# A seven-product form for 3 of 8 pairs of k-tiles in the FFN input products of an encoder block

## The chip, the cores and the metric

The kernel runs on one core of one Trainium2 chip. The metric is the device time of one execution in microseconds, as the median of several runs. A profile of one further execution comes with it; it names the engines PE (TensorE, matmul), PEld (its weight loads), DVE (VectorE), ACT (ScalarE), POOL (GpSimd) and SP (SyncE, here the queue of most transfers).

## The reference

One layer of an encoder block on 256 tokens of width 2048, all float32. Three token mixers run on the normalized input: a dilated window attention, a grouped-query attention with rotary positions, and a cross attention into 256 memory tokens. Each branch is projected to the model width, weighted by a sigmoid gate, summed, projected by `w_o` and added to the input. Behind it stands the part that the change touches, the SwiGLU FFN with an inner width of 5632:

```python
hf = rms_norm(x, g_ffn[layer]) @ w_ffn_in[layer]
x = x + (jax.nn.silu(hf[..., :D_FF]) * hf[..., D_FF:]) @ w_ffn_out[layer]
```

`w_ffn_in` is 2048 x 11264; its left half (a) gives the gate, its right half (b) the value.

## The kernel before

**Number format.** TensorE multiplies in a reduced float32 form. To keep float32 accuracy every operand is split into a high part, rounded to that form, and a low part, the rest. `split` (L72) makes both: ACT copies to the high tile (L75), then DVE subtracts it from the source (L76). A product of two tiles is then three matmuls (L172 to L174): high by high, high by low, low by high.

**Tiling.** The 256 tokens are two row tiles (`T`, `t`) of 128. The model width is 16 k-tiles (`KT`) of 128. Weight columns come in tiles of 512 (`NC`), one PSUM bank wide. `product` (L150) multiplies all tokens by one column tile: it takes one bank per row tile, loads 4 k-tiles (1 MB, `raw`, 3 buffers) at a time on the SP queue (L146), splits them two k-tiles at a time into `whi` and `wlo` (4 buffers each), and issues for each k-tile and row tile the three matmuls, with the activations as the stationary operand and the weights streaming.

**Order.** The kernel is written as one program; a planner orders each engine's instructions at build time by priority (program order) and by its own estimate of when operands and buffers are ready. Each engine then runs its list strictly in order, waiting on semaphores. A buffer of a pool is taken when an earlier tile with the same tag is released.

**The stages.** Memory keys and values, the combined projections with the three attentions beside them, gates and branch projections, the `w_o` products, the FFN. In the `w_o` stage (L476) each of four column tiles is added to the residual `x` (L481), squared for the norm (L482), transposed by TensorE (`transposed`, L212, matmuls at L218), scaled by the gain and split into a quarter of `x1T`, the stationary operand of the FFN.

**The FFN.** Two blocks of column tiles, 6 and 5. For each of the 11 column tiles the kernel computes the product with a (L495), applies silu with the row scale of the norm on ACT (L498), computes the product with b (L499), multiplies on DVE (L501), transposes the result and splits it into `hT` (L505). After a block, four output products with `w_ffn_out` run over the block's `hT`, and DVE adds them to `x` (L513); behind the last block the rows go out.

**Memory.** The eight PSUM banks are two pools of 4: `pmm` for products and `pat` for transposes and attention. SBUF tiles of 8 KB per partition come from the pool `big` (11 buffers) and, from the last gate stage on, `tail` (4); those of 4 KB from `mid` (5).

Of the kernel before, what the change touches and what calls it, by code (L numbers as in the profile page):

```python
# [23 lines left out]
HD = 128  # L24
DFF = 5632
NC = 512
KF = DFF // P
PK, LOAD = 2, 4
# [18 lines left out]
MEM_SLOTS = [("kc", _i) for _i in range(4)] + [("vc", _i) for _i in range(4)]  # L47


@with_exitstack  # L50
def encoder_block(ctx: ExitStack, tc: tile.TileContext, a: dict, out: bass.AP):
    nc = tc.nc
    const = ctx.enter_context(tc.tile_pool(name="const", bufs=1))
    wp = ctx.enter_context(tc.tile_pool(name="wp", bufs=3))
# [4 lines left out]
    pmm = ctx.enter_context(tc.tile_pool(name="pmm", bufs=4, space=bass.MemoryType.PSUM))  # L59
    pat = ctx.enter_context(tc.tile_pool(name="pat", bufs=4, space=bass.MemoryType.PSUM))  # L60

    def s8(shape, name, dt=F32R, pool=None):
        return (pool or big).tile(shape, dt, name=name, tag="s8")

    def s4(shape, name, dt=F32):
        return mid.tile(shape, dt, name=name, tag="s4")

    def at_bank(name):
        return pat.tile([P, NC], F32, name=name, tag="at")


    def split(hi, lo, src, scale=None):  # L72
# [77 lines left out]
    def product(src, lhs, nk, head=(), beside={}):  # L150


        ps = [pmm.tile([P, NC], F32, name="mm") for _ in range(T)]
        k0 = 0
        while k0 < nk:
            n = head[0] if head else min(LOAD, nk - k0)
            head = head[1:]
            if k0 in beside:
                start(beside[k0])
            lhs(k0)  # L160
            raw = load(src, k0, n)
            for b in range(0, n, PK):
                m = min(PK, n - b)
                hi = wp.tile([P, PK, NC], F32R, name="whi", bufs=4)
                lo = wp.tile([P, PK, NC], F32R, name="wlo", bufs=4)
                split(hi[:, :m], lo[:, :m], raw[:, b:b + m])
                for i in range(m):
                    k = k0 + b + i
                    xh, xl = lhs(k)
                    for t in range(T):  # L170
                        c = slice(t * P, (t + 1) * P)
                        nc.tensor.matmul(ps[t], lhsT=xh[:, c], rhs=hi[:, i], start=(k == 0), stop=False)  # L172
                        nc.tensor.matmul(ps[t], lhsT=xh[:, c], rhs=lo[:, i], start=False, stop=False)  # L173
                        nc.tensor.matmul(ps[t], lhsT=xl[:, c], rhs=hi[:, i], start=False, stop=(k == nk - 1))  # L174
                    tick()
            k0 += n
        return ps
# [107 lines left out]
    headT, V = {}, {}  # L285
# [141 lines left out]
    r_m, r_x, r_f = (scales[:, i] for i in range(3))  # L427
# [61 lines left out]


    x1l = lambda k: (x1T[k // 4][:, 0, k % 4], x1T[k // 4][:, 1, k % 4])
    for c0, c1 in ((0, 6), (6, KF // 4)):
        hT = []
        for n in range(c0, c1):
            ap = product(a["w_ffn_a"][n], x1l, KT)  # L495
            sa = s4([P, T, NC], "sa")
            for t in range(T):
                nc.scalar.activation(sa[:, t], ap[t], AF.Silu, scale=r_f[:, 0, t:t + 1])  # L498
            bp = product(a["w_ffn_b"][n], x1l, KT)  # L499
            for t in range(T):  # L500
                nc.vector.scalar_tensor_tensor(sa[:, t], bp[t], r_f[:, 0, t:t + 1], sa[:, t],  # L501
                                               op0=ALU.mult, op1=ALU.mult)
            tl = s8([P, 2, 4, S], "hT", pool=tail if n % 6 < 4 and n < 6 or n > 8 else None)
            hT.append(tl)
            transposed([sa[:, t] for t in range(T)], lambda k, m: (tl[:, 0, k:k + m], tl[:, 1, k:k + m]))  # L505
        for n in range(4):
            op = product(a["w_ffn_out"][n][4 * c0 // PK:4 * c1 // PK],
                         lambda k: (hT[k // 4][:, 0, k % 4], hT[k // 4][:, 1, k % 4]), 4 * (c1 - c0))
            for t in range(T):
                for h in range(2 if c0 and n == 3 else 1):  # L510
                    w = NC if not (c0 and n == 3) else NC // 2
                    o = slice(n * NC + h * w, n * NC + (h + 1) * w)
                    nc.vector.tensor_add(x[t][:, o], op[t][:, h * w:(h + 1) * w], x[t][:, o])  # L513
                    if c0:
                        nc.sync.dma_start(out=out[t * P:(t + 1) * P, o], in_=x[t][:, o])


# [33 lines left out]
def _blocks(w):  # L551

    k, n = w.shape
    return w.reshape(k // P // PK, PK, P, n // NC, NC).transpose(3, 0, 2, 1, 4).reshape(n // NC, -1, P, PK * NC)


def _layout(i):
# [37 lines left out]
```

## Time and profile before

| | |
|---|---|
| median of 3 runs | 1437.51 us (1437.31 to 1438.21) |
| the profiled execution | 1438.22 us, of which the span is 1436.4 us |
| granted TensorE clock, mean | 0.998 |
| TensorE busy | 1416.7 us (99%), 6422 matmuls and transposes |
| VectorE busy | 781.2 us (54%) |
| ScalarE busy | 667.2 us (46%) |
| GpSimd busy | 78.8 us (5%) |
| moved by DMA | 276.98 MB, 193 GB/s over the span |
| FFN input products | 3 x 704 matmuls, 88 loads of 1 MB |

The span goes from the first to the last instruction of the profiled execution; the time of that execution is 1.8 us more. "Busy" adds up the durations of an engine's instructions. Matmuls overlap in the array, so that the duration of one is longer than the step from one to the next, and a TensorE that is shown as busy may still be slowed.

### The profile page before, as it was taken

The numbers are of one execution on the slowest core, as the hardware profiler recorded it, in microseconds if no ns is written. First come the engines' busy times: TensorE is split into PE (matmuls) and PEld (weight loads), VectorE is DVE, ScalarE is ACT, GpSimd is POOL, SyncE is SP. The second block draws the span as 40 slices with busy tenths as digits, with TensorE's granted clock in tenths as the row PEclk, the third lists the DMA queues.
The fourth block names the chain that finished last, engine by engine and source line by source line (L and its number), as shares of the span: only waits on it lengthen the run. The fifth ranks groups of instructions, "written<-read, shape, count | busy, mean of one in ns | idle before, by whom it ended". The sixth has DMA issues, their size and how long they took to land.

```text
span 1436.4 us, 16231 instructions
## 1 busy us (share of the span) xinstructions
PE 1416.7 (99%) x6422; PEld 1170.0 (81%) x6422; DVE 781.2 (54%) x912; ACT 667.2 (46%) x860; POOL 78.8 (5%) x146
## 2 busy tenths in 40 slices
PE   6999999999999999999999999999999999999998
PEld 4778788888888888888888888888888888888887
DVE  5677766744555555555644555545444445554543
ACT  6676555644444444444444444444333444444432
POOL 0013642200000000000000000000000000000000
PEclk9999999999999999999999999999999999999999
DMA  8876445465555556555555555565555555556562
GB/s 294 282 248 204 147 153 173 160 222 197 196 192 194 176 189 213 184 187 177 183 197 186 194 177 204 176 205 177 203 179 203 187 194 179 202 177 204 192 218 88
DMA packets 75772, 276.98 MB, mean 193 GB/s; under 512 B 5232, under 2 KB 7792, under 8 KB 75440
## 3 DMA queue, kind: packets, MB, share of 16 engines
q1 hardware_dynamic: 73248, 271.73, 56.0%
q10 hardware_dynamic: 2448, 4.22, 0.8%
q8 instruction: 50, 0.82, 0.2%
q14 instruction: 26, 0.21, 0.0%
HBM read 273.05 MB, written 2.88 MB: 192 GB/s over the span
## 4 chain that ended last, share of the span: by engine, by line
PE 92%; DMA 3%; POOL 2%; ACT 1%; issue 1%; DVE 1%; SPq 0%; ACTq 0%; DVEq 0%; POOLq 0%
PE mm L173 29%; PE mm L172 29%; PE mm L174 29%; PE tp L218 1%; DMA rawT<-in_xT 1%; DMA rows<-in_x 1%; DMA rows<-in_mem 1%; POOL rot L337 1%; POOL rot L340 1%; POOL rtmp L338 1%; ACT whi L75 0%; PE pT L396 0%; ACT rows L206 0%; PE hT L346 0%; POOL y L320 0%
## 5 line engine op out<-in xcount | busy, mean ns | idle before, releaser
L76 DVE TENSOR_TENSOR wlo<-raw,whi 128x1024 fp32r<-128x1024 f32 (+1 forms) x497 | 614.7, 1239 | 584.9 <-ACT whi L75 582.6
L75 ACT ACTIVATE whi<-raw 128x1024 fp32r<-128x1024 f32 (+1 forms) x497 | 525.5, 1061 | 642.6 <-PE mm L174 616.6
L174 PE MATMUL mm<-whi,x1T 128*128 128x512 f32 x704 | 274.8, 390 | 0.0
L172 PE MATMUL mm<-whi,x1T 128*128 128x512 f32 x704 | 274.8, 390 | 0.0
L173 PE MATMUL mm<-wlo,x1T 128*128 128x512 f32 x704 | 274.1, 389 | 0.0
L173 PE MATMUL mm<-wlo,xT 128*128 128x512 f32 x640 | 250.2, 391 | 1.0 <-DVE wlo L76 1.0
L172 PE MATMUL mm<-whi,xT 128*128 128x512 f32 x640 | 250.5, 392 | 0.1
L174 PE MATMUL mm<-whi,xT 128*128 128x512 f32 x640 | 249.5, 391 | 0.0
L173 PEld LDWEIGHTS mm<-wlo,x1T 128*128 128x128 f32 x704 | 132.2, 188 | 27.2
L174 PEld LDWEIGHTS mm<-whi,x1T 128*128 128x128 f32 x704 | 132.2, 188 | 27.1
L172 PEld LDWEIGHTS mm<-whi,x1T 128*128 128x128 f32 x704 | 132.2, 188 | 26.9
L173 PEld LDWEIGHTS mm<-wlo,xT 128*128 128x128 f32 x640 | 120.2, 188 | 26.1 <-DVE wlo L76 1.4
L172 PEld LDWEIGHTS mm<-whi,xT 128*128 128x128 f32 x640 | 120.1, 188 | 25.3 <-issue 0.8
L174 PEld LDWEIGHTS mm<-whi,xT 128*128 128x128 f32 x640 | 120.2, 188 | 24.4
L173 PE MATMUL mm<-wlo,hT 128*128 128x512 f32 x352 | 137.8, 391 | 0.0
L172 PE MATMUL mm<-whi,hT 128*128 128x512 f32 x352 | 137.7, 391 | 0.0
L174 PE MATMUL mm<-whi,hT 128*128 128x512 f32 x352 | 137.0, 389 | 0.0
L172 PEld LDWEIGHTS mm<-whi,hT 128*128 128x128 f32 x352 | 66.1, 188 | 14.4
L174 PEld LDWEIGHTS mm<-whi,hT 128*128 128x128 f32 x352 | 66.1, 188 | 14.3
L173 PEld LDWEIGHTS mm<-wlo,hT 128*128 128x128 f32 x352 | 66.1, 188 | 13.5
L173 PE MATMUL mm<-wlo,mT 128*128 128x512 f32 x128 | 50.8, 397 | 0.0
L172 PE MATMUL mm<-whi,mT 128*128 128x512 f32 x128 | 50.5, 395 | 0.0
(123 smaller groups left out, 997.5 us busy)
## 6 DMA issues: line engine op xcount, KB each, us to landing
raw<-in_w_gate SPq DMA_DIRECT2D x48, 1024.0 KB, 5.0
raw<-in_w_ffn_a SPq DMA_DIRECT2D x44, 1024.0 KB, 5.0
raw<-in_w_ffn_b SPq DMA_DIRECT2D x44, 1024.0 KB, 5.0
raw<-in_w_ffn_out SPq DMA_DIRECT2D x44, 1024.0 KB, 5.0
raw<-in_w_qkv SPq DMA_DIRECT2D x32, 1024.0 KB, 5.1
raw<-in_w_o SPq DMA_DIRECT2D x16, 1024.0 KB, 5.0
raw<-in_w_br SPq DMA_DIRECT2D x8, 1024.0 KB, 4.9
raw<-in_w_mem SPq DMA_DIRECT2D x15, 512.0 KB, 4.9
```

The source lines that it names most:

```text
L75: nc.scalar.activation(hi, src, AF.Copy)
L76: nc.vector.tensor_sub(lo, src, hi.bitcast(F32))
L172: nc.tensor.matmul(ps[t], lhsT=xh[:, c], rhs=hi[:, i], start=(k == 0), stop=False)
L173: nc.tensor.matmul(ps[t], lhsT=xh[:, c], rhs=lo[:, i], start=False, stop=False)
L174: nc.tensor.matmul(ps[t], lhsT=xl[:, c], rhs=hi[:, i], start=False, stop=(k == nk - 1))
L218: nc.tensor.transpose(tp[:, k * S + t * P:k * S + (t + 1) * P], src[t][:, (2 * h + k) * P:(2 * h + k + 1) * P], ident)
L337: nc.gpsimd.tensor_mul(ov[:, :, :, c], xv[:, :, :, c], cs[0])
L338: nc.gpsimd.tensor_mul(tmp[:, :n], xv[:, :, :, 1 - c], cs[1])
L340: op(ov[:, :, :, c], ov[:, :, :, c], tmp[:, :n])
```

## The change

The columns of a and b that belong together are now taken in one call, `in_seven`, and the weights lie so that one load of 1 MB holds one pair of k-tiles for both halves: `raw[:, 0]` and `raw[:, 1]` are the two k-tiles of a, `raw[:, 2]` and `raw[:, 3]` those of b. A pair of k-tiles, two row tiles and the two halves are a 2 x 2 by 2 x 2 block product, that is 8 products of tiles. For pairs 3 to 7 ("d", direct) these are computed as before, into the banks Y, V (half a) and Z, Q (half b). For pairs 0 to 2 ("s", `SEVEN`) the Winograd form of Strassen's scheme is used, with 7 products on sums of tiles:

- Two products on the plain tiles of a (into X and Y), at step "s".
- Two products on the b half (into W and Z), at step "s": before its split, the first k-tile of a is added onto the loaded first k-tile of b by a DMA from GpSimd's queue that accumulates.
- Three products on further weight sums, `t2`, `t3`, `t4`, which DVE makes at step "s" for all three pairs and which are split and multiplied at the steps "6", "7" (both continue bank X, with a copy by ACT between) and "4" (into V).

The stationary sides of four of the seven are sums of tiles of `x1T`; `stationary_forms` makes them once, on DVE, and splits them. The steps are issued in the order of `ORDER`, for the first column tile of `ORDER0`. At the end of a column tile six DVE operations combine the banks and copies into the two row tiles of a and of b; silu, the product and the transposes follow as before, in place.

Around it: the two PSUM pools are closed before the FFN and opened again as 7 banks for products and 1 for transposes; the FFN has three blocks of 4, 4 and 3 column tiles instead of 6 and 5; every `hT` lies in `tail`.

```diff
+SEVEN = 3
+ORDER = "s0 d3 s1 d4 s2 d5 6 d6 7 d7 4".split()
+ORDER0 = "d3 d4 d5 s0 s1 d6 s2 6 d7 7 4".split()
...
-    for c0, c1 in ((0, 6), (6, KF // 4)):
+    banks.close()
+    pools["mm"] = ctx.enter_context(tc.tile_pool(name="pm2", bufs=7, space=bass.MemoryType.PSUM))
+    pools["at"] = ctx.enter_context(tc.tile_pool(name="pa2", bufs=1, space=bass.MemoryType.PSUM))
+
+    def stationary_forms():
+        fh = s8([P, 4, SEVEN, P], "fh")
+        fl = s8([P, 4, SEVEN, P], "fl")
+        raw = s8([P, 4, SEVEN, P], "fraw", F32)
+        full = s8([P, 2 * SEVEN, S], "ffull", F32)
+        for q in range((SEVEN + 1) // 2):
+            n = min(4, 2 * SEVEN - 4 * q)
+            nc.vector.tensor_add(full[:, 4 * q:4 * q + n], x1T[q][:, 0, :n].bitcast(F32), x1T[q][:, 1, :n].bitcast(F32))
+        b = full.rearrange("p (u k) (t s) -> p k t u s", k=2, t=2)
+        nc.vector.tensor_sub(raw[:, 0], b[:, 0, 1], b[:, 1, 1])
+        nc.vector.tensor_sub(raw[:, 3], b[:, 0, 0], b[:, 0, 1])
+        nc.vector.tensor_sub(raw[:, 1], raw[:, 0], b[:, 0, 0])
+        nc.vector.tensor_add(raw[:, 2], raw[:, 1], b[:, 1, 0])
+        split(fh, fl, raw)
+        return lambda u, f: (fh[:, f, u], fl[:, f, u])
...
+        def mul(b, st, hi, lo):
+            first = b not in ps
+            if first:
+                ps[b] = mm_bank("mm" + b)
+            left[b] -= 1
+            chain = b == "X"
+            stop = left[b] == 0 or chain and left[b] % SEVEN == 0
+            nc.tensor.matmul(ps[b], lhsT=st[0], rhs=hi, start=first, stop=False, skip_group_check=chain)
+            nc.tensor.matmul(ps[b], lhsT=st[0], rhs=lo, start=False, stop=False, skip_group_check=chain)
+            nc.tensor.matmul(ps[b], lhsT=st[1], rhs=hi, start=False, stop=stop, skip_group_check=chain)
...
+        for o in order:
+            if o[0] in "sd":
+                u = int(o[1])
+                raw = wp.tile([P, LOAD, NC], F32, name="raw")
+                nc.sync.dma_start(out=raw.rearrange("p k n -> p (k n)"), in_=src[u])
+            if o[0] == "d":
+                for c in range(2):
+                    hi, lo = halves()
+                    split(hi, lo, raw[:, 2 * c:2 * c + 2])
+                    for k in range(2):
+                        for t in range(T):
+                            mul(("YV", "ZQ")[c][t], at(2 * u + k, t), hi[:, k], lo[:, k])
+                    tick()
+            elif o[0] == "s":
+                hi, lo = halves()
+                split(hi, lo, raw[:, :2])
+                mul("X", at(2 * u, 0), hi[:, 0], lo[:, 0])
+                mul("Y", at(2 * u + 1, 0), hi[:, 1], lo[:, 1])
+                hi, lo = halves()
+                nc.gpsimd.dma_start(out=raw[:, 2], in_=src[u][:, :NC], accum_op=ALU.add)
+                split(hi, lo, raw[:, 2:])
+                mul("W", forms(u, 0), hi[:, 0], lo[:, 0])
+                mul("Z", forms(u, 2), hi[:, 1], lo[:, 1])
+                nc.vector.tensor_add(t2[:, u], raw[:, 2], raw[:, 3])
+                nc.vector.tensor_sub(t3[:, u], t2[:, u], raw[:, 0])
+                nc.vector.tensor_add(t4[:, u], t2[:, u], raw[:, 1])
+                tick()
+                if left["X"] == 2 * SEVEN:
+                    nc.scalar.activation(SA[:, 0], ps["X"], AF.Copy)
+                if left["W"] == 0:
+                    nc.scalar.activation(SA[:, 1], ps["W"], AF.Copy)
+            else:
+                tt, f = {"6": (t2, 1), "7": (t3, 3), "4": (t4, None)}[o]
+                for v in range(0, SEVEN, 2):
+                    n = min(2, SEVEN - v)
+                    hi, lo = halves()
+                    split(hi[:, :n], lo[:, :n], tt[:, v:v + n])
+                    for i in range(n):
+                        u = v + i
+                        mul(dest[o], at(2 * u + 1, 1) if f is None else forms(u, f), hi[:, i], lo[:, i])
+                tick()
+                if o == "6":
+                    nc.scalar.activation(SB[:, 0], ps["X"], AF.Copy)
+                elif o == "7":
+                    nc.scalar.activation(SB[:, 1], ps["X"], AF.Copy)
+        nc.vector.tensor_sub(SB[:, 0], SB[:, 0], SA[:, 1])
+        nc.vector.tensor_sub(SA[:, 1], SA[:, 1], SB[:, 1])
+        nc.vector.tensor_add(SA[:, 0], ps["Y"], SA[:, 0])
+        nc.vector.tensor_add(SB[:, 1], ps["V"], SB[:, 1])
+        nc.vector.tensor_sub(SB[:, 0], ps["Z"], SB[:, 0])
+        nc.vector.tensor_add(SA[:, 1], ps["Q"], SA[:, 1])
+        return (SA[:, 0], SB[:, 1]), (SB[:, 0], SA[:, 1])
+
+    forms = stationary_forms()
+    for c0, c1 in ((0, 4), (4, 8), (8, KF // 4)):
         hT = []
         for n in range(c0, c1):
-            ap = product(a["w_ffn_a"][n], x1l, KT)
-            sa = s4([P, T, NC], "sa")
+            av, bv = in_seven(a["w_ffn"][n], x1l, forms, ORDER0 if n == 0 else ORDER)
             for t in range(T):
-                nc.scalar.activation(sa[:, t], ap[t], AF.Silu, scale=r_f[:, 0, t:t + 1])
-            bp = product(a["w_ffn_b"][n], x1l, KT)
-            for t in range(T):
-                nc.vector.scalar_tensor_tensor(sa[:, t], bp[t], r_f[:, 0, t:t + 1], sa[:, t],
+                nc.scalar.activation(av[t], av[t], AF.Silu, scale=r_f[:, 0, t:t + 1])
+                nc.vector.scalar_tensor_tensor(av[t], bv[t], r_f[:, 0, t:t + 1], av[t],
                                                op0=ALU.mult, op1=ALU.mult)
-            tl = s8([P, 2, 4, S], "hT", pool=tail if n % 6 < 4 and n < 6 or n > 8 else None)
+            tl = s8([P, 2, 4, S], "hT", pool=tail)
...
-        "w_ffn_a": _blocks(f[:, :DFF]), "w_ffn_b": _blocks(f[:, DFF:]),
+        "w_ffn": np.concatenate([_blocks(f[:, :DFF]), _blocks(f[:, DFF:])], -1),
```

The same buffers that held `hT` or attention tiles in `big` now hold the forms (`fh`, `fl`, and for a while `fraw`, `ffull`) and one set of `t2`, `t3`, `t4`.

More of the change, by code (lines that the diff above doesn't have):

```diff
@@ L68, in at_bank, with mm_bank @@
     def at_bank(name):
-        return pat.tile([P, NC], F32, name=name, tag="at")
+        return pools["at"].tile([P, NC], F32, name=name, tag="at")
+    def mm_bank(name="mm"):
+        return pools["mm"].tile([P, NC], F32, name=name, tag="mm")
     def split(hi, lo, src, scale=None):
@@ L150, in product @@
     def product(src, lhs, nk, head=(), beside={}):
-        ps = [pmm.tile([P, NC], F32, name="mm") for _ in range(T)]
+        ps = [mm_bank() for _ in range(T)]
         k0 = 0
@@ L509, in encoder_block @@
             for t in range(T):
-                for h in range(2 if c0 and n == 3 else 1):
-                    w = NC if not (c0 and n == 3) else NC // 2
+                for h in range(2 if last and n == 3 else 1):
+                    w = NC if not (last and n == 3) else NC // 2
                     o = slice(n * NC + h * w, n * NC + (h + 1) * w)
                     nc.vector.tensor_add(x[t][:, o], op[t][:, h * w:(h + 1) * w], x[t][:, o])
-                    if c0:
+                    if last:
                         nc.sync.dma_start(out=out[t * P:(t + 1) * P, o], in_=x[t][:, o])
```

28 lines of the change are left out of this document (25 added, 3 removed).

## The prediction

> **What bounds the kernel now.** I read the head of the page first (busy shares and the chain of waits), then the waits of TensorE, then one FFN column tile in the table of windows, then its instructions by form.
>
> ```profile
> span 1436.4 us, 16231 instructions
> PE 1416.7 (99%) x6422; PEld 1170.0 (81%) x6422; DVE 781.2 (54%) x912; ACT 667.2 (46%) x860; POOL 78.8 (5%) x146
> ...
> PE 92%; DMA 3%; POOL 2%; ACT 1%; issue 1%; DVE 1%; SPq 0%; ACTq 0%; DVEq 0%; POOLq 0%
> ```
> ```profile
> PE mm L172 <- ACT memT L78: 11.9, 2, 6.2
> PE hT L346 <- POOL rot L340: 1.7, 2, 1.4
> PE mm L173 <- DVE wlo L76: 1.0, 1, 1.0
> PE mm L174 <- DVE memT L79: 0.2, 1, 0.2
> ```
>
> TensorE has 92% of the chain and is busy 99% of the span. The four rows are all its recorded waits: 14.8 us, mostly at the start (memT). In the FFN it waits for nothing. So TensorE instructions taken out of the FFN come off the span, unless the change makes TensorE wait.
>
> ```profile
> 840.28 0.66 PE tp L218 x6
> 884.74 0.65 PE tp L218 x6
> ```
> ```profile
> 880.04 0.39 PE L173 MATMUL mm<-wlo,x1T 128*128 128x512 f32 x1
> 880.26 0.39 PE L174 MATMUL mm<-whi,x1T 128*128 128x512 f32 x1
> 880.49 0.39 PE L172 MATMUL mm<-whi,x1T 128*128 128x512 f32 x1
> ```
> ```profile
> 840.28:884.74 44.46, 44.46 (x202) 36.82 (x201) 22.22 (x20) 19.21 (x20) 0.00 (x0) 1.00 0.56 190
> ```
> ```profile
> L76 DVE TENSOR_TENSOR wlo<-raw,whi 128x1024 fp32r<-128x1024 f32 x16 | 19.6, 1226 | 20.9 <-ACT whi L75 20.7
> L75 ACT ACTIVATE whi<-raw 128x1024 fp32r<-128x1024 f32 x16 | 17.0, 1061 | 22.3 <-PE mm L174 22.3
> L501 DVE SCALAR_TENSOR_TENSOR sa<-mm,scales,sa 128x512 f32<-128x512 f32 x2 | 1.4, 744 | 0.0
> L498 ACT ACTIVATE sa<-mm,scales 128x512 f32<-128x512 f32 x2 | 1.4, 690 | 1.0 <-PE mm L174 1.0
> L76 DVE TENSOR_TENSOR hT<-tp,hT 128x512 fp32r<-128x512 f32 x2 | 1.3, 686 | 1.4 <-ACT hT L75 1.4
> L75 ACT ACTIVATE hT<-tp 128x512 fp32r<-128x512 f32 x2 | 1.1, 596 | 2.0 <-PE tp L218 2.0
> ```
>
> The first pair gives the period of a column tile, from one set of transposes to the next: 44.46 us. The listed 390 ns of a matmul is pipelined; the starts 880.04 and 880.49 are two steps, so a matmul costs 0.227 us, and 192 of them 43.5 us of the period. In that window VectorE (DVE) is busy 22.22 us, ScalarE (ACT) 19.21, GpSimd (POOL) 0, and the granted clock is 1.00. The by-form rows show the ring: ACT waits for TensorE (22.3 us) to free one of the four whi/wlo pairs, DVE waits for ACT (20.7), TensorE waits for neither. So splits run ahead by the depth of the ring, four pairs, and no more.
>
> **The change, part by part.**
>
> *Fewer products.* In 3 of 8 pairs of k-tiles, 8 products become 7. A product is 3 matmuls, and there are 11 column tiles: 3 x 11 x 3 = 99 matmuls, each with its own weight load as now. 99 x 0.227 = **-22.4 us**. A tile's TensorE time becomes 44.46 - 9 x 0.227 = 42.4 us.
>
> *More work on DVE and ACT.*
>
> ```profile
> L465 DVE TENSOR_TENSOR mg<-mg,sg 128x512 f32<-128x512 f32 x16 | 10.3, 681 | 0.0
> ```
>
> Per tile there are now 6 full splits for the seven-form pairs, 10 for the five direct pairs, and a full and a half one for each of the three weight sums: 19 full and 3 half, where there were 16 full. DVE also makes 9 weight sums and 6 output sums of 128x512, priced by the row above. DVE: 22.22 + 3 x 1.226 + 3 x 0.686 + 15 x 0.681 = 38.2 us, which is 90% of the new 42.4. ACT: 19.21 + 3 x 1.061 + 3 x 0.596 + 4 copies x 0.690 = 26.9 us, 64%. DVE stays below TensorE, so on average the work is hidden; what decides is whether it is hidden at each place. The ring is the limit, since DVE cannot use slack beyond four pairs.
>
> In the new order a seven-form step takes 2.72 us of TensorE and up to 4.5 of DVE (two splits, three sums), a direct step 5.44 and 2.45; they alternate, so 8.16 stands against 6.95. The narrow place is the seam between two tiles. Set 0 where TensorE ends the last direct step (d7). Without a wait it then does "4" (9 matmuls, to 2.04), the next tile's s0 (12, to 4.76) and starts d3, whose second matmul needs its wlo at 4.99. Bank Z is complete at -0.68, Q at 0, V at 2.04, each plus 0.16 for the end of the last matmul (0.39 - 0.227). DVE must do from -0.52: Z 0.68, Q 0.68, the gate product 0.74, the split of s0's second half 1.23, V 0.68, d3's first split 1.23: 5.24, so it is done at 4.72, 0.27 us ahead. The sum on Y, the two differences that read no bank, and s0's three weight sums can be done before, during d6 and d7, where DVE does 4.9 of 10.9 us; the last of the three sums waits only for the old t4 to be split, at about -3. The lower end is 0 per tile; with all three sums in the seam (2.04) it is 1.8 per tile, 20 us. I take 0.1 per tile, **+1 us**, because the walk fits and the trace has a stretch with as full a DVE:
>
> ```profile
> 100.00:200.00 100.00, 98.27 (x509) 82.47 (x509) 72.78 (x125) 59.97 (x131) 48.47 (x81) 1.00 0.55 180
> ```
>
> There DVE has 72.8% and GpSimd runs beside it, and all waits for DVE listed above come to 1.2 us. But 90% is more than this trace shows.
>
> *The sum by DMA.* Three times per tile GpSimd's queue, empty in the FFN (0.00, x0, in the window), adds 256 KB onto a loaded tile; behind it wait ACT's split, DVE's split and sums in order, and TensorE's W and Z products. No accumulating transfer is in the trace. The nearest rows:
>
> ```profile
> raw<-in_w_ffn_a SPq DMA_DIRECT2D x44, 1024.0 KB, 5.0
> ...
> rawT<-in_memT ACTq DMA_DIRECT2D x8, 256.0 KB, 4.3
> rows<-in_mem SPq DMA_DIRECT2D x4, 512.0 KB, 8.0
> ...
> rows<-in_x SPq DMA_DIRECT2D x4, 512.0 KB, 13.2
> ```
>
> The budget: s2's load takes the buffer that d3 leaves. On the same clock d3's second split ends at about 6.7 (4.72, then the second gate product 0.74 and 1.23), the load lands 5.0 later at 11.7. TensorE comes to s2's second half at 0.93 (transposes) + 2.04 + 2.72 + 5.44 + 2.72 + 5.44 + 1.36 = 20.65; less 1.06 and 1.23 for its splits, 18.4. So the accumulate has 6.6 us. For s1 (buffer left by d7 at -5.0, landed at 0.0, needed at 10.2) it is 10.2, for s0 more. Lower end 4.3 (the same bytes, plain), upper 13.2 (twice the bytes, which is what it reads, in the kernel's first stage). I take 5, nearest the 256 KB row: **0**. At 13.2 it would be late by 6.6 and 3.0 in each tile, 106 us in all.
>
> *The banks.* All eight PSUM banks are given back before the FFN and dealt anew, 7 and 1. A tile of a new pool waits for every user of the pools whose bytes it takes, so the first FFN matmul waits for the whole end of the w_o stage, which now runs beside it:
>
> ```profile
> 701.04 1.28 DVE L481 TENSOR_TENSOR x<-mm,x 128x512 f32<-128x512 f32 x2
> ...
> 701.36 0.39 PE L172 MATMUL mm<-whi,x1T 128*128 128x512 f32 x1
> ...
> 702.52 0.61 ACT L482 ACTIVATE junk<-x 128x512 f32<-128x512 f32 x1
> ...
> 703.13 0.62 ACT L482 ACTIVATE junk<-x 128x512 f32<-128x512 f32 x1
> ...
> 706.57 0.82 PE L218 MATMUL tp<-ident,x 128*128 128x128 f32 x6
> 707.10 0.84 ACT L78 ACTIVATE x1T<-tp,gT 128x256 fp32r<-128x256 f32 x2 [1.71 <-PE tp L218]
> ...
> 710.19 0.87 DVE L79 SCALAR_TENSOR_TENSOR x1T<-tp,gT,x1T 128x256 fp32r<-128x256 f32 x2
> ```
>
> The additions end at 702.3, the transposes then take 1.1 us while ACT squares (to 703.8), ACT's four x1T halves end at 703.8 + 2 x 0.84 = 705.5, DVE's last one 0.48 later, 706.0. TensorE starts at about 706.1 instead of 701.36, and 0.93 us of transposes lies inside: **+3.8 us**, once. Lower end 0, if banks come free one by one. The idle could also cost clock:
>
> ```profile
> 151.46 0.66 PE L346 MATMUL hT<-ident,rot 128*128 128x128 f32 x4 [1.40 <-POOL rot L340]
> ```
> ```profile
> 19.75 0.80 PE L172 MATMUL mm<-whi,memT 128*128 128x512 f32 x1 [5.77 <-ACT memT L78]
> 20.34 0.63 PE L173 MATMUL mm<-wlo,memT 128*128 128x512 f32 x1
> 20.77 0.63 PE L172 MATMUL mm<-whi,memT 128*128 128x512 f32 x1
> ...
> 24.32 0.40 PE L173 MATMUL mm<-wlo,memT 128*128 128x512 f32 x1
> ```
>
> After 5.77 us without work the step was 0.43 us until 24.3, some 2.2 us lost; after 1.40 us the clock stayed 1.00. The longest pause here, from 703.5 to 706.1, is 2.6, nearer 1.40: I take 0 and keep 2.2 for the range. The Trainium skill (TensorE: Matmul & The Clock Gate, part 1) puts the fall to half rate after an idle window of about 3.4 us; by it too the sum has no such term.
>
> *The stationary forms and the third block.* Two sums, four of three quarters of 512, and a split of 128x1536 are about 6 us of DVE. They need the first two quarters of x1T, done by the second of four w_o tiles, and the first seven-form step comes behind three direct ones: 0, under two w_o tiles (2 x 96 x 0.227 = 43.6 us); bare they would cost 6. Three blocks instead of two add 8 output sums (0.68 each) under out products where DVE is half idle: 0. SP issues as many 1 MB loads as before, in one queue; GpSimd's transfers pass no other.
>
> **Sum**, against the profiled execution (1438.2 us, span 1436.4): -22.4 + 1 + 0 + 3.8 = -17.6, so 1420.6. The median of the runs is 0.7 below that execution: **1420 us**, 1.2% faster. Its own range is 1416 to 1427.
>
> **Rivals.**
> 1. *The accumulate comes late* (ends slower). Place: s2's W and Z products in every tile, then s1's. It decides against the change beyond 17.6 / 11 = 1.6 us over the budget, that is from 8.2 us on. At 10 us it costs 11 x 3.4 = 37: **1457**. For it: no row shows such a transfer, and DMA already carries a 0.56 share. Against: the plain one lands in 4.3. The Trainium skill (SBUF — State Buffer, "SBUF: two separate sides") says that descriptors of a GpSimd-issued DMA are written by GpSimd itself and starve while VectorE holds the port pair they share; its example grows from 0.62 to 3.1 us. By an estimate from it the 5 would be 7.5 and the time about 1430. Chance 0.15.
> 2. *DVE sets the pace at the seam*: the sums of s0 stand in it, 1.8 us per tile, 11 x 1.8 = 20: **1439**, no change. For it: 90% load, in-order queue, 0.27 us to spare. Against: the early stretch above. Chance 0.15, half of it with only part of the sums there, 1427 to 1434.
> 3. *The banks cost nothing*, because they are handed over one by one: **1416**. Chance 0.08.
>
> **How the numbers follow.** The forecast has 0.62. About 0.2% (3 us) is what a measurement of this kernel can tell from no change. Faster: 0.62 + 0.08 + 0.07 of rival 2 + 0.01 of rival 1 = 0.78. Same: 0.05 + 0.02 = 0.07. Slower: 0.03 + 0.12 = 0.15. The range runs from 1414.5, where rival 3 also loses nothing at the seam (1437.5 - 22.4 = 1415.1), to 1441, which takes in rival 2; what is left out above is rival 1.
>
> **What would show it.** Right: 99 fewer x1T-type matmuls at a step of 0.227; a tile period near 42.5 us; DVE near 38 busy in it; one TensorE wait of 3 to 5 us at the start of the FFN, released by DVE's x1T split; the accumulate landing in 4 to 6. Wrong: a TensorE wait for whi or wlo once per tile at the seam (rival 2), or at the W products with ACT waiting for the accumulating transfer (rival 1), or no wait at the start of the FFN (rival 3); or a half clock behind it.

## The result and the profile after

The changed kernel takes 1507.49 us, the median of 4 runs (1497.92 to 1512.32), against 1437.51 us before. The ratio is 1.048 with a 95% interval of 1.0425 to 1.053. The prediction was 1420 us with a range of 1414.5 to 1441. It was wrong, and on the other side: 70 us slower instead of 17 us faster.

The head of the page of the changed kernel, its chain of waits, and the granted clock:

```profile
span 1504.3 us, 16612 instructions
PE 1427.1 (95%) x6323; PEld 1159.7 (77%) x6323; DVE 941.5 (63%) x1158; ACT 738.4 (49%) x971; POOL 107.4 (7%) x179
...
PE 61%; DMA 22%; DVE 11%; issue 3%; POOL 2%; ACT 2%; POOLq 0%; ACTq 0%; DVEq 0%; SPq 0%
DMA raw<-in_w_ffn 19%; PE mm L184 17%; PE mm L185 17%; PE mm L183 17%; DVE wlo L87 7%; ACT whi L86 1%; DVE t L587 1%; DVE t L589 1%; DVE t L588 1%; DMA rows<-in_mem 1%; PE mmV L550 1%; PE mmV L549 1%; PE tp L229 1%; POOL rot L348 1%; PE mmZ L550 1%
```
```profile
core 0: 1504.3 us, clock 0.982
```

The 99 matmuls are gone (6422 to 6323), but TensorE's share of the chain fell from 92% to 61%. Transfers into `raw` hold 19% of it now (11% the accumulating ones of GpSimd, 8% the loads of 1 MB; the row doesn't tell them apart, the queues of the trace do), and DVE 11%. The waits of TensorE, in the columns waiter, releaser, us in total, times, longest:

```profile
PE mmX L549 <- DVE wlo L87: 19.0, 7, 3.4
...
PE mmW L548 <- ACT whi L86: 10.9, 7, 2.4
PE mmY L549 <- DVE wlo L87: 8.9, 5, 3.6
PE mmY L548 <- DVE rs_h L96: 5.6, 1, 5.6
PE mmZ L549 <- DVE wlo L87: 3.5, 2, 1.7
PE mmW L549 <- DVE wlo L87: 3.0, 8, 0.7
```

Before, the FFN had none. All but one of these rows are products that wait for a split of ACT or DVE; the other, 5.6 us, is the start of the FFN. One step deeper, in all waits of the same kernel, stand those that ACT and DVE have for `raw` (of ACT's 85.2 us, 73.3 are for the accumulating transfer, the rest for loads), and in the list of DMA issues the transfer itself (bytes and median time to landing); the last line is the spread of its time to landing:

```profile
DVE t L587 <- DMA raw<-in_w_ffn: 125.0, 31, 6.9
...
ACT whi L86 <- DMA raw<-in_w_ffn: 85.2, 19, 7.6
```
```profile
raw<-in_w_ffn SPq DMA_DIRECT2D x88, 1024.0 KB, 5.2
...
raw<-in_w_ffn POOLq DMA_DIRECT2D x33, 256.0 KB, 5.2
```
```profile
DMA to landing us min/median/max: 4.0/5.2/8.8
```

DVE's first weight sum (L587) reads what the accumulating transfer writes. It waits for it 31 times of 33, 125 us in all, or 11.4 us per column tile. The table of windows shows two tiles, each from the stall at step s2 to the next such stall:

```profile
1066.12:1117.63 51.51, 46.61 (x192) 36.61 (x191) 35.95 (x41) 25.49 (x30) 2.59 (x3) 0.93 0.57 178
1117.63:1168.33 50.70, 46.48 (x193) 36.72 (x191) 35.94 (x41) 25.61 (x30) 2.59 (x3) 0.93 0.56 181
```

The period of a tile is 51 us, where 42.4 was forecast and 44.46 stood before. DVE is busy for 36.0 of them. In a period of 42.4 us DVE would have had 6.4 us to wait in; it waits 11.4 for this one transfer. The clock in these windows is 0.93: the waits also cost speed.

From 701 us to the end I took, for each TensorE instruction, the time to the start of the next and compared it with the full step (0.2267 us, 0.11 for a transpose). The excess is 63.3 us where a wait is recorded, 15.0 us in 75 matmuls that ran at half clock (0.42 to 0.44 us apart), and 13.3 us of smaller differences, most of them longer steps right behind a wait or a transpose. Before, the same sums are 0, 0 and 1.8.

How one tile goes, in the order of time: DVE, GpSimd, ACT and TensorE around one seam between two tiles.

```profile
1066.26 0.69 DVE L587 TENSOR_TENSOR t<-raw 128x512 f32<-128x512 f32 x1 [5.31 <-DMA raw<-in_w_ffn]
...
1084.79 0.69 DVE L587 TENSOR_TENSOR t<-raw 128x512 f32<-128x512 f32 x1 [6.78 <-DMA raw<-in_w_ffn]
1085.40 1.22 DVE L87 TENSOR_TENSOR wlo<-t,whi 128x1024 fp32r<-128x1024 f32 x1
...
1117.63 0.69 DVE L587 TENSOR_TENSOR t<-raw 128x512 f32<-128x512 f32 x1 [5.17 <-DMA raw<-in_w_ffn]
```
```profile
1077.85 0.86 POOL L583 DMA_DIRECT2D raw<-in_w_ffn  x1 [18.76 <-DMA raw<-in_w_ffn]
...
1109.66 0.86 POOL L583 DMA_DIRECT2D raw<-in_w_ffn  x1 [12.42 <-DVE wlo L87]
```
```profile
1117.71 2.00 ACT L86 ACTIVATE whi<-raw 128x1024 fp32r<-128x1024 f32 x2 [6.63 <-DMA raw<-in_w_ffn]
```
```profile
1086.67 0.79 PE L549 MATMUL mmX<-wlo,fh 128*128 128x512 f32 x1 [3.31 <-DVE wlo L87]
1087.26 0.63 PE L550 MATMUL mmX<-whi,fl 128*128 128x512 f32 x1
1087.69 0.63 PE L548 MATMUL mmX<-whi,fh 128*128 128x512 f32 x1
```

The sum at 1084.79 belongs to the next tile's s0. The load of that s0 lands at 1077.29, the accumulate is issued at 1077.85 and lands 6.9 us later. The sum stands in DVE's list ahead of the split of step "7" (1085.40), so DVE stands idle for 6.78 us with a split behind it for which TensorE is waiting (3.31 us), and then TensorE runs at half clock. Five of the seven waits of X for DVE are of this kind, in step "7" (15.6 of the 19.0 us). At s2 (1109.66 to 1117.63, 8.0 us) both ACT and DVE stand idle, 6.63 and 5.17 us.

The start of the FFN has a wait too, as was forecast, but longer:

```profile
702.97 0.87 PE L229 MATMUL tp<-ident,x 128*128 128x128 f32 x6 [0.16 <-DVE x L492]
709.46 0.77 PE L548 MATMUL mmY<-whi,x1T 128*128 128x512 f32 x1 [5.61 <-DVE rs_h L96]
710.02 0.63 PE L549 MATMUL mmY<-wlo,x1T 128*128 128x512 f32 x1
...
713.01 0.62 PE L550 MATMUL mmY<-whi,x1T 128*128 128x512 f32 x1
713.44 0.43 PE L548 MATMUL mmV<-whi,x1T 128*128 128x512 f32 x1
```

### The profile page after: what moved, and what is told of

Its sections match the earlier page's. It is cut to its first block, busy times and chain, and to the rows that moved or that the text cites. A ratio compares the mean times of both kernels' runs of the same rounds, so it can differ in the third digit from the quotient of the medians.

```text
span 1504.3 us, 16612 instructions
## 1 busy us (share of the span) xinstructions
PE 1427.1 (95%) x6323; PEld 1159.7 (77%) x6323; DVE 941.5 (63%) x1158; ACT 738.4 (49%) x971; POOL 107.4 (7%) x179
## 4 chain that ended last, share of the span: by engine, by line
PE 61%; DMA 22%; DVE 11%; issue 3%; POOL 2%; ACT 2%; POOLq 0%; ACTq 0%; DVEq 0%; SPq 0%
DMA raw<-in_w_ffn 19%; PE mm L184 17%; PE mm L185 17%; PE mm L183 17%; DVE wlo L87 7%; ACT whi L86 1%; DVE t L587 1%; DVE t L589 1%; DVE t L588 1%; DMA rows<-in_mem 1%; PE mmV L550 1%; PE mmV L549 1%; PE tp L229 1%; POOL rot L348 1%; PE mmZ L550 1%
## 5 line engine op out<-in xcount | busy, mean ns | idle before, releaser
L583 POOL DMA_DIRECT2D raw<-in_w_ffn x33 | 28.6, 868 | 1105.5 <-DVE wlo L87 682.2
L587 DVE TENSOR_TENSOR t<-raw 128x512 f32<-128x512 f32 x33 | 22.8, 692 | 125.0 <-DMA raw<-in_w_ffn 125.0
L86 ACT ACTIVATE whi<-t 128x1024 fp32r<-128x1024 f32 x66 | 55.5, 842 | 29.1 <-PE mmX L550 27.5
L549 PE MATMUL mmY<-wlo,x1T 128*128 128x512 f32 x143 | 59.0, 413 | 9.0 <-DVE wlo L87 8.9
L548 PE MATMUL mmY<-whi,x1T 128*128 128x512 f32 x143 | 59.3, 414 | 7.3 <-DVE rs_h L96 5.6
L87 DVE TENSOR_TENSOR wlo<-t,whi 128x1024 fp32r<-128x1024 f32 x66 | 62.0, 953 | 1.0
L550 PE MATMUL mmY<-whi,x1T 128*128 128x512 f32 x143 | 57.5, 402 | 0.0
L548 PE MATMUL mmV<-whi,x1T 128*128 128x512 f32 x143 | 57.3, 401 | 0.0
```

What stands on the lines that cost most here:

```text
L86: nc.scalar.activation(hi, src, AF.Copy)
L87: nc.vector.tensor_sub(lo, src, hi.bitcast(F32))
L548: nc.tensor.matmul(ps[b], lhsT=st[0], rhs=hi, start=first, stop=False, skip_group_check=chain)
L549: nc.tensor.matmul(ps[b], lhsT=st[0], rhs=lo, start=False, stop=False, skip_group_check=chain)
L550: nc.tensor.matmul(ps[b], lhsT=st[1], rhs=hi, start=False, stop=stop, skip_group_check=chain)
L583: nc.gpsimd.dma_start(out=raw[:, 2], in_=src[u][:, :NC], accum_op=ALU.add)
```

## The experiments

The theory: the accumulating transfer comes late, DVE and ACT stand idle in their lists for it, and everything else is a consequence. Rivals: DVE with its 36 us of work per tile is too slow by itself; the banks cost most of it. All ratios are to the kernel before, whose medians were 1437 to 1439 us in every set of runs. An edit also lets the planner order the lists anew. In run 2, TensorE, DVE and ACT keep the changed kernel's order in the FFN; in most other runs it differs in places, so that such a run prices its edit together with the new order.

**1. The transfer left out**, and with it the sum; the first k-tile of b stays as loaded.

```diff
-                nc.gpsimd.dma_start(out=raw[:, 2], in_=src[u][:, :NC], accum_op=ALU.add)
```


> The changed kernel without the accumulating transfer (the addition of a's first k-tile onto b's is left out; everything else stays). Theory A (the accumulate comes late and VectorE and ScalarE, in order, stand behind it): of the 68 us between the spans, about 60 us are TensorE waits inside the column tiles and about 21 us matmuls at half clock behind such waits; both go, and what is left is the saving of 22, the start of the FFN (6.5 and 2 of clock) and small change: 1425 to 1435 us. VectorE then waits for no transfer in the FFN. Theory B (VectorE at 90% cannot keep up at the seams, whatever the transfer does): VectorE has the same work, 1490 to 1510 us.

Measured: 1434.35 us, 0.9975 (0.9964 to 0.9986). DVE has the same work as in the changed kernel, and 73 us are gone, 3 more than the change had cost. The two longest waits of TensorE in its FFN:

```profile
PE mmY L548 <- DVE rs_h L96: 5.6, 1, 5.6
PE mmY L549 <- DVE wlo L87: 2.1, 7, 0.3
```

So the loss hangs on the transfer and the order made around it, not on DVE's load. The wait at the start of the FFN stays and is a separate cost.

**2. A plain copy in its place**, same queue, same 256 KB, nothing added.

```diff
-                nc.gpsimd.dma_start(out=raw[:, 2], in_=src[u][:, :NC], accum_op=ALU.add)
+                nc.gpsimd.dma_start(out=raw[:, 2], in_=src[u][:, :NC])
```


> The same 256 KB, from the same queue (GpSimd's), at the same place, but as a plain copy that overwrites b's tile instead of adding to it (so the sum is left out). If what is late is any transfer issued by GpSimd behind a load: landing stays at 4 to 8 us and the time at 1490 to 1510 us. If what is late is the accumulation (its second read of the same bytes): landing falls to 2.5 to 4.3 us and the time to 1430 to 1460 us. Theory B: 1490 to 1510 us with either landing.

Measured: 1482.88 us, 1.029 (1.0253 to 1.0327).

```profile
DMA to landing us min/median/max: 3.2/5.1/8.0
```

That the transfer adds, and doesn't only copy, is a third of the loss (1507.5 - 1482.9 = 25 us of the 73); a plain one of the same size at this place already costs 1482.9 - 1434.4 = 48.5. Two thirds of the loss are there with any second transfer of this size between the load and the split.

**3. The sum by DVE**, one `tensor_add` of 128x512 in place of the transfer.

```diff
-                nc.gpsimd.dma_start(out=raw[:, 2], in_=src[u][:, :NC], accum_op=ALU.add)
+                nc.vector.tensor_add(raw[:, 2], raw[:, 2], raw[:, 0])
```


> The sum made by VectorE instead of the transfer: three more operations of 0.68 us per column tile, VectorE at about 40.2 of 42.4 us. Theory A: no transfer stands behind another any more, so 1430 to 1445 us, with more small waits than without the sum. Theory B: more work on the engine that sets the pace, about 22 us more than the changed kernel, 1520 to 1535 us.

Measured: 1432.25 us, 0.9954 (0.9937 to 0.9971). DVE gets still more work, 963.7 us instead of 941.5, and the kernel is 75 us faster than the changed one. That settles it against the rival of DVE's load. The wait at the start of the FFN is there (6.2 us).

**4. The pools' waits tile by tile**: the two reopened PSUM pools with `reuse_waits="tile"`, all else as changed.

> The changed kernel, with the two new PSUM pools opened so that each bank waits only for its own earlier users, not for all users of the old pools. Theory: the wait at the start of the FFN (5.6 us recorded, 6.5 us of step, and some 2 us of half clock) goes and nothing else changes: 8 to 9 us faster than the changed kernel, 1494 to 1502 us. Rival (the wait only moves, because x1T's last quarter is late anyway): no change, 1503 to 1511 us.

Measured: 1498.82 us, 1.0413 (1.0386 to 1.0441). The median is 8.7 us below the changed kernel's, as the theory had it, but not for its reason (the two ranges overlap, 1495.58 to 1501.42 and 1497.92 to 1512.32): the wait at the start did not go. It only moved, from the bank Y to the bank V, 4.9 us:

```profile
PE mmV L548 <- DVE rs_h L96: 4.9, 1, 4.9
```

**5. The sum by DVE and the pools left open**: X and W take banks of the transposes' pool of 4, the other four banks that of the products.

```diff
-    banks.close()
-    pools["mm"] = ctx.enter_context(tc.tile_pool(name="pm2", bufs=7, space=bass.MemoryType.PSUM))
-    pools["at"] = ctx.enter_context(tc.tile_pool(name="pa2", bufs=1, space=bass.MemoryType.PSUM))
...
-                ps[b] = mm_bank("mm" + b)
+                ps[b] = (at_bank if b in "XW" else mm_bank)("mm" + b)
...
-                nc.gpsimd.dma_start(out=raw[:, 2], in_=src[u][:, :NC], accum_op=ALU.add)
+                nc.vector.tensor_add(raw[:, 2], raw[:, 2], raw[:, 0])
```


> The sum on VectorE, as in e2_dve_sum, and the PSUM pools left as they were: X and W take banks of the pool for transposes, Y, V, Z and Q those of the products. e2_dve_sum had one wait of 6.2 us at the start of the FFN, 6.9 of step, and some 2 us of half clock behind it. Theory (that wait is the price of the new pools alone): it goes, 8 to 9 us less than e2_dve_sum, 1421 to 1426 us. Rival (four banks for Y, V, Z, Q with none to spare make each column tile wait for the sums of the tile before): 11 waits of 1 to 2 us at the seams, 1430 us or more.

Measured: 1423.72 us (1422.04 to 1425.63), 0.9896 (0.9881 to 0.9911). This is the seven-product form without its two faults, 1.0% faster than the kernel before and the fastest of all runs here. The first FFN product now starts at 700.92 us and waits for nothing, and one tile in the middle of the FFN:

```profile
1004.00:1046.00 42.00, 42.00 (x190) 34.65 (x189) 37.31 (x44) 25.41 (x30) 0.00 (x0) 1.00 0.57 200
```

In this stretch TensorE has no gap, DVE is busy 37.3 of 42.0 us (89%), and the clock is 1.00. A DVE of 89% does carry this stage, so long as nothing in its list is late.

**6. The kernel before with its pools reopened, 4 and 4**, in the same order. **7. The same with the two pools opened in the other order**, so that the products' pool takes the transposes' banks. The lines are those of run 7; run 6 opens `mm` first.

```diff
+    banks.close()
+    pools["at"] = ctx.enter_context(tc.tile_pool(name="pa2", bufs=4, space=bass.MemoryType.PSUM))
+    pools["mm"] = ctx.enter_context(tc.tile_pool(name="pm2", bufs=4, space=bass.MemoryType.PSUM))
```


> The kernel before, with nothing changed but that its two PSUM pools are closed before the FFN and opened again, 4 and 4. By the prediction's step this costs 3.8 us, 1441 us; by what the changed kernels show (6.5 us of step, matmuls at 0.43 us for some 4 us behind it) 8 to 9 us, 1445.5 to 1447. If the wait is due to something else in the new FFN (the forms, the order of its splits): 0 to 2 us.

> The kernel before, with its PSUM pools closed ahead of the FFN and reopened as 4 and 4 in the other order, so that the products' new pool lies on the banks that the last transposes use. Theory: the first FFN product then waits for the last split of the transposed quarter, as in the changed kernel: a wait of 5 to 6 us at the start of the FFN, about 2 us more at half clock behind it, 1444 to 1447. Rival: a product waits only when all of one pool is taken; then no wait, 1437 to 1440 as with the unswapped order.

Measured: 1438.72 us, 1.0007 (0.9997 to 1.0016), for the same order, which was not what I expected; and 1444.26 us, 1.0045 (1.003 to 1.006), for the other. In the first, the new products' pool lies on the old products' banks alone, and the wait is not there. In the second it lies on the transposes' banks:

```profile
703.10 0.88 PE L219 MATMUL tp<-ident,x 128*128 128x128 f32 x6 [0.15 <-DVE x L482]
707.07 0.48 PE L173 MATMUL mm<-whi,x1T 128*128 128x512 f32 x1 [3.10 <-DVE rs_t L93]
707.38 0.60 PE L174 MATMUL mm<-wlo,x1T 128*128 128x512 f32 x1
707.77 0.63 PE L175 MATMUL mm<-whi,x1T 128*128 128x512 f32 x1
```

Closing a pool costs nothing by itself. The price comes with new tiles that overlap a bank whose reader is late: 6.5 us here (1444.26 against 1437.79), with a half clock behind it. The changed kernel's pool of 7 of the 8 banks has to take at least three of the transposes' four.

**8. The three weight sums on GpSimd** (`t2`, `t3`, `t4`), the transfer kept, so that DVE's splits don't stand behind a sum that waits.

```diff
-                nc.vector.tensor_add(t2[:, u], raw[:, 2], raw[:, 3])
-                nc.vector.tensor_sub(t3[:, u], t2[:, u], raw[:, 0])
-                nc.vector.tensor_add(t4[:, u], t2[:, u], raw[:, 1])
+                nc.gpsimd.tensor_add(t2[:, u], raw[:, 2], raw[:, 3])
+                nc.gpsimd.tensor_sub(t3[:, u], t2[:, u], raw[:, 0])
+                nc.gpsimd.tensor_add(t4[:, u], t2[:, u], raw[:, 1])
```


> The accumulating transfer stays; only the three weight sums t2, t3, t4 behind it go to GpSimd, so that VectorE's queue no longer holds an operation that waits for the transfer directly. Theory (half of the loss is VectorE standing behind the transfer with work that TensorE needs): the waits of TensorE for wlo in banks X and Y (28 us in the changed kernel) go, the waits for whi at bank W, where ScalarE stands behind the transfer, stay or grow; about half of the loss comes back, 1460 to 1480 us. Rival (the transfer delays the data itself, and the order of the queues is of no matter): no change, 1500 to 1510 us. If GpSimd's own additions hold up its next transfer: slower than 1510.

Measured: 1495.19 us, 1.039 (1.035 to 1.043), 12 us better than the changed kernel, far from the half of the loss that was expected. The waits moved:

```profile
PE mmW L548 <- ACT whi L86: 21.7, 9, 3.1
...
PE mmW L549 <- DVE wlo L87: 10.4, 19, 0.8
```
```profile
POOL t L587 <- DMA raw<-in_w_ffn: 162.6, 31, 7.9
...
ACT whi L86 <- DMA raw<-in_w_ffn: 102.4, 25, 9.0
```

The waits of X for DVE are nearly gone (19.0 to 0.6 us), those of W for ACT doubled (10.9 to 21.7). GpSimd's list also issues the transfers, and the three sums take it 5.6 us of each s step (69.4 + 67.0 + 47.1 us over 33, rows at the end), so the next transfer's issue can have them ahead of it. In three of the 33 steps the issue comes 2 to 3.6 us behind the landing of the load; in the other 30 it comes within 1.2 us, so this is not what held the run back.

**9. The half that is added to is loaded first**: the 1 MB load of each s step cut in two, b half first.

> The accumulating transfer stays, but the load of a seven-form pair is cut in two, with the b half first, so that the transfer can start 1.5 to 2.5 us earlier (a 512 KB load against a 1 MB one). Theory A, as a dose: each of the about two waits per column tile shrinks by that much, and some stay below the length at which the clock falls: 1465 to 1490 us. If the transfer is slow because it runs beside the loads: it now runs beside the second half, lands later by as much as it starts earlier, and the time stays at 1495 to 1510 us.

Measured: 1503.04 us, 1.0439 (1.0415 to 1.0463). No gain, for neither of the two reasons that were put down. The b half does land earlier and the transfer behind it is not longer (median 4.7 us against 5.2), so that the sum at s2 is there 9.6 to 11.7 us after its load's issue, where it took 10.2 to 14.4 in the changed kernel. The waits of X for DVE go (19.0 to 0.7 us), but the other products wait more: 15.8 us for the splits of Y, 11.2 for those of Z, and 11.2 us of the transposes for DVE's gate products. An earlier sum by itself, then, did not buy time back; how the lateness is passed on from list to list stays open.

Runs 8 and 9 left it open why the transfer is late at all. The loads are limited by three `raw` buffers. At s2 in the tile shown the buffer is free at 1104.14 us (the last split of d3), its load lands 4.9 us later, and the sum is there at 1117.6. A buffer is held for load, transfer and splits in turn.

**10. The transfer kept, the pools left open.** **11. The same, with a fourth `raw` buffer** that step s2 alone uses; four blocks of column tiles instead of three make room for it. **12. As 11, but with the sum by DVE**, which tells what the buffer and the smaller blocks do by themselves.

```diff
+                if o == "s2":
+                    raw = tail.tile([P, LOAD, NC], F32, name="raw4", bufs=1)
+                else:
+                    raw = wp.tile([P, LOAD, NC], F32, name="raw")
...
-    for c0, c1 in ((0, 4), (4, 8), (8, KF // 4)):
+    for c0, c1 in ((0, 3), (3, 6), (6, 9), (9, KF // 4)):
```


> The changed kernel with its accumulating transfer, but with the two PSUM pools of 4 left open as they were before (X and W take banks of the transposes' pool). Theory: the wait at the start of the FFN and the half clock behind it are a cost of the reopened pools alone, 5.6 + 2 us, and independent of the late sums; so the run is 7 to 10 us below the changed kernel, 1493 to 1503, and its waits inside the column tiles stay near 55 us. Rival: the late sums give the start another wait in its place, so that less than 3 us is gained, about 1506.

> Same as the kernel with the pools left open and the accumulating transfer kept, but step s2 loads into a fourth buffer of its own (blocks of 3, 3, 3 and 2 column tiles make the room for it), so that its load can start before the last split of d3. Theory 'the sum is late because the buffer is late': load, accumulate and splits in turn hold a buffer too long for three of them; with a fourth the waits inside the tiles fall from about 55 us to under 20, the time to 1435 to 1460. Rival 'the order of the queues is late': the sums still stand in ACT's and DVE's lists ahead of other splits and wait for a transfer of 7 to 8 us; then s0 and s1 stay late and the time stays above 1475.

> The kernel with the fourth buffer, four smaller blocks and the pools left open, with the first of the four sums made by DVE and not by the transfer. It tells what the blocks and the buffer do by themselves. Theory: they do nothing where no sum comes late, so it runs like the kernel with the DVE sum and three buffers, 1420 to 1428; then the 41 us that the fourth buffer gave are those of the late transfer, and the 35 us that are left there against this run are what the transfer still costs with four buffers. Rival: the smaller blocks move work by themselves (8 more output sums for DVE, other seams); then it differs by more than 5 us, upward if the sums cost, downward if the buffer helps.

| transfer or DVE | buffers | median, us | ratio |
|---|---|---|---|
| transfer (10) | 3 | 1500.72 (1493.72 to 1512.31) | 1.0446 (1.0395 to 1.0496) |
| transfer (11) | 4 | 1459.26 (1455.82 to 1461.36) | 1.0148 (1.0129 to 1.0168) |
| DVE (5) | 3 | 1423.72 (1422.04 to 1425.63) | 0.9896 (0.9881 to 0.9911) |
| DVE (12) | 4 | 1428.64 (1427.05 to 1431.36) | 0.9926 (0.991 to 0.9943) |

The fourth buffer takes 41 us off the kernel with the transfer, and nothing off the one without: that one gets 5 us slower, 0.6 us above what I had allowed for. In run 10 the wait at the start is gone, but two products now wait for DVE to read out a bank (Q 8.2 us, V 5.3 us), which the rival of run 5 had named and run 5 does not show. In run 11 TensorE's waits in the FFN come to 25 us, where under 20 was expected. The waits of run 10, and then of run 11, in all waits of each:

```profile
DVE t L584 <- DMA raw<-in_w_ffn: 117.0, 30, 6.8
...
ACT whi L86 <- DMA raw<-in_w_ffn: 47.2, 14, 7.2
```
```profile
DVE t L591 <- DMA raw<-in_w_ffn: 59.2, 23, 6.7
...
ACT whi L86 <- DMA raw<-in_w_ffn: 21.2, 6, 6.4
```
```profile
DMA to landing us min/median/max: 4.1/5.2/7.6
```

ACT's waits fell by half, DVE's by about half or, if 18.8 us that the trace of run 11 puts down to no releaser belong to them, by a third; the median time to landing is nearly the same (5.3 us in run 10). So the larger part of the loss can be had back by a buffer: with three of them the load that the transfer must wait for can't start earlier. Of the 77 us that the transfer costs with three buffers (1500.7 - 1423.7), 31 are left with four (1459.3 - 1428.6). I did not follow how those 31 divide between the steps and the order of DVE's list.

## Why the prediction was wrong, step by step

| step | forecast, us | measured, us | from |
|---|---|---|---|
| 99 matmuls fewer | -22.4 | -22.4 | 6422 to 6323, full step 0.227 |
| more work on DVE and ACT | +1 | +8 | run 5: -14.4 in all |
| the sum by DMA | 0 | +77 | run 10 less run 5 |
| the banks | +3.8 | +6.5 to 8.5 | run 7; changed kernel less run 10 (6.8, the ranges overlap); run 3 less run 5 (8.5) |
| sum | -17.6 | +70 | changed kernel |

*Fewer products* was right. Run 5 is 14.4 us below the kernel before (1438.1 us in the same set of runs): -22.4, and 8.0 that it loses. The reckoning of TensorE's steps finds 8.6 of it (5.2 where a wait is recorded, none at half clock, 5.2 of smaller differences, against 0, 0 and 1.8 before).

*DVE and ACT*: right in kind. The 38.2 us of DVE in a tile were 36.0 in the changed kernel, and 37.3 of 42.0 (89%) in run 5, which has three sums more. The size was off: 8 us instead of 1, inside the bounds of 0 and 20. Rival 2 as it was put, that DVE sets the pace at the seam by its load alone, fell with runs 1, 3 and 5.

*The sum by DMA* is **the step that failed**: "So the accumulate has 6.6 us ... I take 5 ...: 0". Two things in it were wrong, and one held.
- The landing time. The median over all, 5.2 us, is the 5 that I took. But by step the medians are 6.4 us at s0, 4.1 at s1 and 8.0 at s2, where the budget of 6.6 was least. The spread (4.0 to 8.8) counts, not the median.
- What held is the walk up to the transfer: s2's load was to land 11.7 us behind the end of d7, and in six of the eight tiles that follow another tile directly it landed 11.6 to 13.8 us behind it. Issued 0.6 us after that, the sum was there at 19.4 to 23.1, past the 18.4 of the forecast. So the three buffers left no room for a transfer of 8 us; run 11 priced the missing buffer at 41 us.
- Whom it makes wait. I counted a late transfer as a wait of the W and Z products. It is first a wait of DVE and ACT, in whose fixed lists other splits stand behind it. Since DVE was to be busy 38.2 of 42.4 us, by the forecast's own numbers it had 4.2 us per tile to lose, for all waits together. Waits of 11.4 could not be made up.

Rival 1 named the transfer, and the waits at W with ACT waiting for it are in the trace. But its price was too small: by it the 8.0 us at s2 cost 11 x 1.4 = 15 us, and those at s0 and s1 nothing. Here the transfer cost 77. The larger wait, at X, is a wait for DVE, as in rival 2, but not at its place: it stands in step "7", ahead of d7, where the seam of rival 2 begins behind it, and DVE is not busy there but stands at the sum of the next s0. Neither rival was the case as it was put.

The sentence from the Trainium skill (SBUF — State Buffer, "SBUF: two separate sides"), that the descriptors of a GpSimd-issued transfer starve while VectorE holds the port pair that it shares with GpSimd, isn't what is seen here: a transfer of 6.86 us (1077.85) has DVE busy for 0.2 us of it, and one of 4.13 us, the s0 transfer of the second tile, has DVE busy throughout. What goes with the time is the 1 MB loads under way beside it. Of the 33 transfers, 18 take 4.0 to 5.5 us, and all but two of them have at most 3.9 us of a load beside them; 15 take 6.4 to 8.8 us, and each has more than 5 us of loads beside it. In five of the six s0 transfers of 6.4 us and more the first packet moves 4.0 to 4.6 us after the issue, where it moves after 1.6 us in those of 4.0 to 4.3. The plain copies of run 2 show the same spread, 3.2 to 8.0. That the loads cause it was not tested by itself.

*The banks*: the mechanism held. The wait is one, at the start of the FFN, and by the times it ends with DVE's last work on `x1T` (the releaser that the row names, `rs_h`, is the small operation that follows it; in run 3 the row names `x1T`). The size was off twice. I had priced the clock at 0, for a pause of 2.6 us; the pause is 5.61 and the step 0.43 us until 713.4, some 2 us. (Even 2.6 would not have been safe: see the last section.) And the pause is longer because the work of *the forms*, priced at 0 as hidden, stood inside it:

```profile
704.38 1.82 DVE L516 TENSOR_TENSOR ffull<-x1T 128x1024 f32<-128x1024 f32 x2
...
706.97 0.55 DVE L518 TENSOR_TENSOR fraw<-ffull 128x384 f32<-128x384 f32 x1
...
708.83 0.48 DVE L90 SCALAR_TENSOR_TENSOR x1T<-tp,gT,x1T 128x256 fp32r<-128x256 f32 x1
```

DVE makes the full tiles and three of the form sums (1.82 and 3 x 0.55, 3.5 us) between the pieces of the last quarter of `x1T`, which so ends at 709.31 instead of the 706.0 of the forecast. The cover that I had named, two `w_o` tiles, was there; the order of DVE's list did not use it. Without the forms, in run 7, the price is the 6.5 us. Rival 3 fell.

The two changes that repair the failed step and the banks, run 5, come to 1423.7 us, inside the forecast's own range of 1416 to 1427. That is in part luck: there the banks cost 0 instead of 3.8, and DVE and ACT 8 instead of 1.

## What to carry to other kernels

A transfer put between a load and its first reader lengthens the time that each buffer of the ring is held; price it by the ring (load + transfer + readers against buffers x period per load), and by its slowest landing beside the other traffic, not by its median. A wait on an engine that runs its list in order costs that engine's free time, so an engine that is planned to 90% has no more than the last 10% of the period to wait in, for all waits together. Where 0.7 us on a busy engine replaces a transfer of 5 us off it, the busy engine can be the cheaper place.

## What the runs showed of the hardware that I had not expected

- A transfer of 256 KB issued by GpSimd took 4.0 to 8.8 us where it accumulates and 3.2 to 8.0 us where it only copies, so that its time differs far more from one place to the next than by the adding.
- The clock fell to half after pauses of TensorE shorter than I had thought. In the FFN of the changed kernel it did so nine times, for 3.41 or 6.83 us each; one fall came with a pause of 2.45 us, while one of 2.74 us brought none:

```profile
780.54 0.50 PE L548 MATMUL mmW<-whi,fh 128*128 128x512 f32 x1 [2.45 <-ACT whi L86]
800.44 0.50 PE L549 MATMUL mmX<-wlo,fh 128*128 128x512 f32 x1 [2.74 <-DVE wlo L87]
```

  The nine falls lie whole multiples of 3.413 us apart. Counted in such steps, the one ahead of each fall held 1.95 to 3.19 us without a matmul, and no other step at full clock more than 1.67 (in runs 4 and 10 the two groups overlap, between 1.4 and 1.9 us). So where a pause lies in its step decides too. The Trainium skill (TensorE: Matmul & The Clock Gate, part 1) puts the fall at an idle window of about 3.4 us; the trace has it after less. In the changed kernel it adds 15.0 us to the 63.3 us of waits.
- GpSimd's sums of 128x512 float32 took 1.4 to 2.1 us in run 8, where DVE's take 0.69:

```profile
L588 POOL TENSOR_TENSOR t<-t,raw 128x512 f32<-128x512 f32 x33 | 69.4, 2102 | 2.4
L589 POOL TENSOR_TENSOR t<-t,raw 128x512 f32<-128x512 f32 x33 | 67.0, 2031 | 8.0 <-DVE wlo L87 8.0
L587 POOL TENSOR_TENSOR t<-raw 128x512 f32<-128x512 f32 x33 | 47.1, 1428 | 169.4 <-DMA raw<-in_w_ffn 162.6 <-DVE SB L613 6.8
```
